# Router stage: second norm's shift by adding transfers, f32 router logits, another bank for the last projection, low parts later

## The chip, the cores and the metric

The kernel runs on one core of a Trainium2 chip. The core has five instruction queues that matter here: PE (TensorE, the matrix unit; PEld is its weight load), DVE (VectorE), ACT (ScalarE), POOL (GpSimd) and SP (SyncE, which here only issues transfers). Each works through its own instructions in order and waits for semaphores of the others. PSUM, where PE writes its results, has eight banks. The metric is the device time of one execution in microseconds (us), as the median of several runs.

## The reference

One layer of a diffusion transformer over 1024 tokens of width 1024, with a router and 16 experts. Each expert takes the 128 tokens that have the highest affinity for it.

```python
h = modulate(rmsnorm(x, g_mix), sh1, sc1)
... windowed attention and a short convolution over h @ w_in ...
x = x + gt1 * (concat([att, conv]) @ w_out)             # output projection

h2 = modulate(rmsnorm(x, g_ffn), sh2, sc2)              # second norm: r*g*(1+sc2) + sh2
aff = softmax(h2 @ w_router)                            # (1024, 16), float32
g, idx = top_k(aff.T, 128)                              # each expert picks 128 tokens
xs = h2[idx]                                            # gathered rows
a, u = xs @ w_gate, xs @ w_up
y = (silu(a) * u) @ w_down * g
x = x + gt2 * segment_sum(y, idx)                       # adds into the rows of the tokens
return rmsnorm(x, g_final)
```

## The kernel before

The kernel goes through the layer in stages. After the attention, a **router stage** goes over 8 tiles of 128 tokens (t = 0 to 7), and then an **expert stage** over 16 experts of three weight matrices each.

**The router stage.** `project(t)` multiplies tile t by `w_out` in 48 matmuls of 512 columns (L878; each product is split into a high part and low parts, three passes in all), adds the residual `xres` on DVE (L883, one operation for each half) and takes the root mean square. While PE works through `project(t)`, the work of the tile before it is woven in: `route(t-1)` turns `xres` by 8 PE transposes into bank `ph` (L951), copies it out of PSUM, multiplies it by the router's weights into logits `pl`, and takes the softmax into `aff`. Beside this, `finish_h2` makes the rows of the second norm: `h2 = x*S2` (`gained`, L887), then `h2*rstd + B2` (L933), and SP stores them to a DRAM tensor `h2_d`, 128 rows for each tile. S2 and B2 are the second norm's scale and shift as rows in SBUF.

For tiles 0 to 6 the logits are made in two steps: ACT copies `ph` as rounded high parts, DVE takes what is left as low parts (`x2s`, L956, two operations), PE multiplies both by the router's weights with the tokens as columns (`plT`, L970, 8 matmuls), ACT copies that out, and PE turns it back with two float32 matmuls (`pl`, L977). Tile 7, the last, is done otherwise: ACT copies `ph` as it is and PE multiplies it in plain float32 (L964, 8 matmuls, each of which shows as two records in the trace).

**Top 128 by sorting.** DVE holds the best 128 affinities of each of the 16 experts so far in a tile `L`. `sort(t0, n)` sorts the affinities of n tiles: PE turns them into a PSUM tile `pa` in bank p1(1), DVE copies that into `sa` (L1050, called the evict below) and then runs eight rounds of MAX8 and MATCH_REPLACE (L1057, L1059), followed by half cleaners (pairs of max and min, L1020 and L1021). `merge(t)` takes the maximum of `L` and the sorted list (L1077) and cleans `L` again with such pairs. Tiles 0 to 2 are sorted together, then 3 and 4, then 5, 6 and 7 alone. After `merge(7)`, `thr` is the smallest of the 128 (L1228). From it come a mask, the places of the chosen tokens, `idx` (L1275) and the gather of the rows of expert 0 from `h2_d` (POOL, L1310), the transposes of these rows (L1286) and the first expert matmul.

**The last tile.** For t = 7 the projection is split, so that the first half of the columns is ready early: 24 matmuls of 512 columns (L878), then two parts c = 0 and c = 1 with 24 matmuls of 256 columns each (L915). Part c = 0 writes to a half of bank pair p2(0); part c = 1 writes to bank p1(1), which is the bank of `pa`.

**The first weights.** The weights of expert 0 are split into a high part by ACT (L1145) and a low part by DVE (L1148) for each k of 8. `pre_split` does this ahead of the expert stage: k = 0, 1 and 2 whole, and the high part of k = 3. The low part of k = 3 stands between the mask of expert 1 and its `idx`.

**What sets the order.** In this stretch PE, SP, ACT and POOL work in the order in which the code is written out (a manual schedule); for DVE a scheduler places the instructions, and code marked as of high priority goes first.

Of the kernel before, what the change touches and what calls it, by code (L numbers as in the profile page):

```python
# [18 lines left out]
D = 1024  # L19
# [13 lines left out]
NW4 = 3  # L33

# [51 lines left out]
def tile_layer(ctx, tc, x, c, cx, c_ctx, w_ada, b_ada, g_mix, w_in, conv_w, sink, w_out, g_ffn,  # L86
# [751 lines left out]
    wmem = work.tile([128, 384], F32R, tag="mp", name="wrs")  # L838
    wrs, ident2 = shaped(wmem, (KC, 2, NE)), wmem[:32, 256:272].bitcast(F32)
    nc.vector.tensor_copy(wrs[:, :, 0], wr)  # L840
    nc.vector.tensor_tensor(wrs[:, :, 1], wr, wrs[:, :, 0].bitcast(F32), op=OP.subtract)
    nc.vector.tensor_tensor(wmem[:32, 256:272], ident[:32, 0:16], ident[:32, 16:32], op=OP.add)

    fold, sign = wmem[:, 272:336].bitcast(F32), wmem[:, 336:337].bitcast(F32)
    nc.vector.tensor_tensor(wmem[:, 272:336], ident[:, 0:64], ident[:, 64:128], op=OP.add)
# [16 lines left out]
    def project(t):  # L862
# [22 lines left out]
        def gained(cols):  # L885

            nc.vector.tensor_tensor(h2_of[t][:, cols], xt[:, cols], S2[:, cols], op=OP.mult)  # L887

        if t < NT - 1:
# [7 lines left out]
            gained(slice(0, D))  # L897
        else:
# [10 lines left out]
            po2 = [p2(0, "po")[:, 0], p1(1, "po")]  # L909
# [20 lines left out]
    def finish_h2(t):  # L930
        h2 = h2_of.pop(t)
        x2_of.pop(t)
        nc.vector.scalar_tensor_tensor(h2, h2, rstd[:, t:t + 1], B2, op0=OP.mult, op1=OP.add)  # L933
        h2_done[t] = h2
        if t < NT - 2:
            store_h2(t)
# [6 lines left out]
    def turn_x2(t, g, ks=None):  # L943
        if t < NT - 1:
            x2T_of[t, g] = (wm, w4)[g]("x2s", (4, 2, 128), F32R)
        elif g == 0:
            x2T_of[t] = wm("x2T")
        ks = ks or range(4 * g, 4 * g + 4)
        ph = p1(2 + ks[0] // 2 % 2 if t == NT - 1 else 2 + g, "ph")[:, 0:128 * len(ks)]
        for i, k in enumerate(ks):  # L950
            nc.tensor.transpose(ph[:, i * 128:(i + 1) * 128], x2_of[t][:, k * 128:(k + 1) * 128], ident)  # L951
        if t < NT - 1:
            hi, lo = [x2T_of[t, g][:, :, i] for i in range(2)]
            ph = ph.rearrange("p (a b) -> p a b", a=4)
            nc.scalar.copy(hi, ph)
            nc.vector.tensor_tensor(lo, ph, hi.bitcast(F32), op=OP.subtract)  # L956
        else:
            nc.scalar.copy(x2T_of[t][:, ks[0] * 128:(ks[-1] + 1) * 128], ph)
# [7 lines left out]
    def logits_T(t):  # L966

        pl = p1(0, "plT")
        for k in range(KC):
            mm(pl[:2 * NE, :256], wrs[:, k].rearrange("p a b -> p (a b)"),  # L970
               x2T_of[t, k // 4][:, k % 4].rearrange("p a b -> p (a b)"), start=k == 0, stop=k == KC - 1)
        lgT = work.tile([32, 256], F32, tag="up", name="lgT")
        nc.scalar.copy(lgT, pl[:32, :256])
        yield 0.8
        pl_of[t] = p1(0, "pl")
        for i in range(2):
            mm(pl_of[t][:, :NE], lgT[:, i * 128:(i + 1) * 128], ident2, start=i == 0, stop=i == 1)  # L977
# [223 lines left out]
    with order_of:  # L1201
# [19 lines left out]
        pre_split((2,))  # L1221
        split_rows("g", 0, 3, (0,))
# [307 lines left out]
```

## Time and profile before

| | us |
|---|---|
| median of 3 runs | 1177.36 (1175.39 to 1178.09) |
| the profiled execution, its own time | 1176.17 |
| its span in the trace | 1174.3 |
| PE busy | 1063.7 (91%) |
| DVE busy | 982.9 (84%) |
| ACT busy | 767.9 (65%) |
| POOL busy | 349.0 (30%) |

The busy shares are means over stages which have different limits. The router stage lies at about 440 to 580 us of the span, the expert stage at about 590 to 1130 us. In the profile's slices PE is at 9 tenths or more through the whole expert stage, and at less in the router stage's last part. All start times below are microseconds from the start of the span.

### The profile page before, as it was taken

The page shows a single profiled execution, that of the slowest core. Times are in us where ns is not written, and L with a number is a line of the kernel's source. Part 1 is how long each engine was busy: PE and PEld are TensorE (multiplying, and loading weights), DVE is VectorE, ACT ScalarE, POOL GpSimd, SP SyncE. Part 2 cuts the span into 40 slices and gives each one's busy share as a digit, 9 for nine tenths or more (in the row PEclk, how much of TensorE's full clock was granted, in tenths as well). Part 3 has the DMA queues.
Part 4 walks back from the last instruction along what each step waited for, and adds up shares of the span by engine and source line. Part 5 has one row for each costly group of instructions (what it writes and reads, how often), then busy time and mean ns, then how long its engine had stood idle before and what let it go on. Part 6 is the DMA issues. An engine that isn't in the chain of part 4 may idle for free.

```text
span 1174.3 us, 15578 instructions
## 1 busy us (share of the span) xinstructions
PE 1063.7 (91%) x5458; PEld 873.2 (74%) x5458; DVE 982.9 (84%) x1678; ACT 767.9 (65%) x1064; POOL 349.0 (30%) x288
## 2 busy tenths in 40 slices
PE   6786889999899998997399999999999999999982
PEld 2675667888787877776278888888888888888861
DVE  7887455887877786599879999999999999999985
ACT  7565545766666744232167888788888778788863
POOL 0457671211303031221204333223333223331022
PEclk9898999999999999999589999999999999999996
DMA  9644540100101175437579999999999999999646
GB/s 377 225 162 143 170 136 19 33 23 1 54 1 37 25 291 205 146 116 277 208 277 369 385 393 389 390 389 397 404 388 390 390 389 387 411 392 388 245 157 254
DMA packets 89638, 288.69 MB, mean 246 GB/s; under 512 B 6916, under 2 KB 20688, under 8 KB 88536
## 3 DMA queue, kind: packets, MB, share of 16 engines
q1 hardware_dynamic: 84808, 270.40, 60.6%
q0 software_dynamic: 4752, 17.30, 5.6%
q8 instruction: 43, 0.70, 0.2%
q14 instruction: 35, 0.29, 0.1%
HBM read 266.69 MB, written 20.99 MB: 245 GB/s over the span
## 4 chain that ended last, share of the span: by engine, by line
PE 71%; DVE 12%; DMA 7%; ACT 4%; issue 4%; POOL 1%; POOLq 0%; ACTq 0%; DVEq 0%; SPq 0%
PE pg L1300 15%; PE pu L1300 14%; PE py L1300 13%; PE po L878 5%; PE ps_cv L731 3%; PE ps_cv L730 3%; PE ps_cv L732 3%; PE pt L622 2%; PE po_att L613 2%; DMA xt<-in_x_dram 2%; PE ps_s L565 1%; PE xTp L1286 1%; PE ps_s L563 1%; PE hTtp L1286 1%; DMA wa<-in_w_ada_dram 1%
## 5 line engine op out<-in xcount | busy, mean ns | idle before, releaser
L1148 DVE TENSOR_TENSOR whl<-raw,whl 128x1024 fp32r<-128x1024 f32 x384 | 455.8, 1226 | 29.3 <-ACT whl L1145 18.5
L1145 ACT CAST whl<-raw 128x1024 fp32r<-128x1024 f32 x384 | 400.4, 1054 | 100.9 <-PE pu L1300 35.5
L1300 PE MATMUL pg<-whl,xT 128*128 128x512 f32 x768 | 187.0, 396 | 2.3 <-DVE whl L1148 2.3
L1300 PE MATMUL pu<-whl,xT 128*128 128x512 f32 x768 | 180.8, 391 | 0.0
L1300 PEld LDWEIGHTS pg<-whl,xT 128*128 128x128 f32 x768 | 142.7, 189 | 32.3 <-DVE whl L1148 3.2
L1300 PE MATMUL py<-whl,hTt 128*128 128x512 f32 x720 | 165.9, 389 | 0.0
L1300 PEld LDWEIGHTS pu<-whl,xT 128*128 128x128 f32 x768 | 143.1, 188 | 29.3
L1300 PEld LDWEIGHTS py<-whl,hTt 128*128 128x128 f32 x720 | 135.1, 188 | 28.3 <-DVE whl L1148 0.3
L1265 POOL TENSOR_SCALAR oh<-iota,pos 128x128 bf16<-128x128 f32 x108 | 103.7, 974 | 9.6 <-DVE pos L1250 9.1
L1358 POOL DMA_INDIRECT acc_d<-yt,idx x15 | 38.6, 2570 | 196.4 <-DVE yt L1346 196.4
L730 PE MATMUL ps_cv<-hTh,wcs 128*128 128x512 f32 x192 | 81.2, 423 | 0.0
L1310 POOL DMA_INDIRECT xr<-h_d,idx x16 | 21.8, 1361 | 189.7 <-DVE gate_w L1276 189.7
L463 POOL TENSOR_TENSOR acc<-acc,wmod 128x1024 f32<-128x1024 f32 x28 | 69.1, 2484 | 30.2 <-ACT wmod L461 29.8
L625 ACT CAST pth<-pt 128x512 fp32r<-128x512 f32 (+1 forms) x88 | 46.1, 524 | 46.1 <-PE pt L622 46.1
L731 PE MATMUL ps_cv<-hTl,wcs 128*128 128x512 f32 x192 | 76.1, 396 | 0.0
L732 PE MATMUL ps_cv<-hTh,wcs 128*128 128x512 f32 x192 | 76.0, 396 | 0.0
L626 DVE TENSOR_TENSOR pth<-pt,pth 128x512 fp32r<-128x512 f32 (+1 forms) x88 | 53.9, 614 | 20.2 <-ACT pth L625 19.0
L878 PE MATMUL po<-woh,ah 128*128 128x512 f32 x240 | 69.3, 403 | 0.6 <-ACT woh L223 0.6
L711 POOL TENSOR_TENSOR wcs<-wcr,wcs 128x1024 fp32r<-128x1024 f32 x12 | 28.6, 2390 | 110.4 <-ACT wcs L710 87.7
L578 ACT ACTIVATE sm<-sm,negm 128x640 f32<-128x640 f32 (+1 forms) x64 | 51.6, 807 | 3.9 <-DVE negm L577 3.8
L575 DVE CUSTOM_DVE_ANT_0 sm<-ps_s,maskt,sink 128x640 f32<-128x640 f32 (+1 forms) x56 | 48.4, 864 | 6.9 <-PE ps_s L565 6.3
L878 PEld LDWEIGHTS po<-woh,ah 128*128 128x128 f32 x240 | 44.4, 191 | 9.6 <-ACT woh L223 1.0
(292 smaller groups left out, 1843.2 us busy)
## 6 DMA issues: line engine op xcount, KB each, us to landing
raw<-in_w_gate_dram SPq DMA_DIRECT2D x64, 1024.0 KB, 10.1
raw<-in_w_up_dram SPq DMA_DIRECT2D x64, 1024.0 KB, 8.7
raw<-in_w_down_dram SPq DMA_DIRECT2D x64, 1024.0 KB, 10.2
wmod<-in_w_ada_dram SPq DMA_DIRECT2D x32, 512.0 KB, 3.8
wa<-in_w_ada_dram SPq DMA_DIRECT2D x8, 1024.0 KB, 5.4
wcr<-in_w_in_dram SPq DMA_DIRECT2D x12, 512.0 KB, 3.8
xt<-in_x_dram SPq DMA_DIRECT2D x4, 1024.0 KB, 20.6
wor<-in_w_out_dram SPq DMA_DIRECT2D x4, 1024.0 KB, 5.0
```

What stands on the lines that cost most here:

```text
L463: nc.gpsimd.tensor_tensor(acc, acc, wt, op=OP.add)
L575: nc.vector.tensor_tensor_reduce(dst, src, mk, op0=OP.add, op1=OP.max, scale=1.0, scalar=sink8[:, h:h + 1], accum_out=mx[:, b, h:h + 1])
L578: nc.scalar.activation(sm, sm, AF.Exp, bias=negm[:, b, h:h + 1], scale=0.125, accum_out=esum[:, b, h:h + 1])
L626: nc.vector.tensor_tensor(pth[:, 1, :n], pt[:, :n], pth[:, 0, :n].bitcast(F32), op=OP.subtract)
L730: mm(ps, wsp[:, 0, k], hi, start=k == 0, stop=False)
L731: mm(ps, wsp[:, 0, k], lo, start=False, stop=False)
L732: mm(ps, wsp[:, 1, k], hi, start=False, stop=k == KC - 1)
L878: mm(po[n], a, wo[k // 4, n][j][:, k % 4], start=first, stop=last)
L1145: nc.scalar.copy(w[:, 0], t[:, k % 2])
L1148: low = nc.vector.tensor_tensor(w[:, 1], t[:, k % 2], w[:, 0].bitcast(F32), op=OP.subtract)
L1265: nc.gpsimd.tensor_scalar(oh[:, t], iota1, pos[:, t, 0, e:e + 1], None, op0=OP.is_equal)
L1300: mm(ps[n], a_hl[:, a, k], w[:, j, n * 512:(n + 1) * 512], start=first, stop=last)
```

## The change

It has four parts.

1. **The second norm's shift.** For tiles 0 to 5 (`NADD = 6`) the rows of `h2_d` are first filled with B2 by six SP stores, early in the stage. `finish_h2` then makes `x*rstd*S2` in one DVE operation, and POOL adds these rows into `h2_d` by an indirect transfer with the row numbers `tokrow` (six small DVE operations). `gained` (L887) and SP's store of the tile are gone for these tiles. Tiles 6 and 7 stay as they were.
2. **The logits of tiles 0 to 6** are made as those of tile 7 were: ACT copies `ph` to `x2T`, PE multiplies in float32. L956, `plT`, its copy and the turn back are gone.
3. **The banks of the last projection.** Part c = 0 takes the second bank of the tile's own pair (`po[1]`), part c = 1 takes what c = 0 had. The bank of `pa` is used by `sort` alone.
4. **The low parts.** `pre_split` makes only the high parts of k = 0 to 3. The low parts of k = 0, 1 are written after the mask of expert 1, those of k = 2, 3 after `place` of the other experts.

```diff
+NADD = 6
...
+    tokrow = consts.tile([128, NT], I32, name="tokrow")
+    for t in range(NADD):
+        nc.vector.tensor_scalar(tokrow[:, t:t + 1], tokid, float(128 * t), None, op0=OP.add)
+        nc.sync.dma_start(h2_d[t * 128:(t + 1) * 128, :], B2)
...
-            gained(slice(0, D))
+            if t >= NADD:
+                gained(slice(0, D))
...
-            po2 = [p2(0, "po")[:, 0], p1(1, "po")]
+            po2 = [po[1], p2(0, "po")[:, 0]]
...
     def finish_h2(t):
-        h2 = h2_of.pop(t)
-        x2_of.pop(t)
-        nc.vector.scalar_tensor_tensor(h2, h2, rstd[:, t:t + 1], B2, op0=OP.mult, op1=OP.add)
-        h2_done[t] = h2
-        if t < NT - 2:
-            store_h2(t)
+        h2, xt = h2_of.pop(t), x2_of.pop(t)
+        if t < NADD:
+            nc.vector.scalar_tensor_tensor(h2, xt, rstd[:, t:t + 1], S2, op0=OP.mult, op1=OP.mult)
+            nc.gpsimd.indirect_dma_start(out=h2_d[:, :], out_offset=bass.IndirectOffsetOnAxis(ap=tokrow[:, t:t + 1], axis=0),
+                                         in_=h2, in_offset=None, compute_op=OP.add)
+        else:
+            nc.vector.scalar_tensor_tensor(h2, h2, rstd[:, t:t + 1], B2, op0=OP.mult, op1=OP.add)
+            h2_done[t] = h2
...
-        if t < NT - 1:
-            hi, lo = [x2T_of[t, g][:, :, i] for i in range(2)]
-            ph = ph.rearrange("p (a b) -> p a b", a=4)
-            nc.scalar.copy(hi, ph)
-            nc.vector.tensor_tensor(lo, ph, hi.bitcast(F32), op=OP.subtract)
-        else:
-            nc.scalar.copy(x2T_of[t][:, ks[0] * 128:(ks[-1] + 1) * 128], ph)
+        nc.scalar.copy(x2T_of[t][:, ks[0] * 128:(ks[-1] + 1) * 128], ph)
...
-            yield 1.3
-            yield from logits_T(t)
+            yield 1.6
+            logits(t, range(0, 4))
+            yield 0.9
+            logits(t, range(4, 8))
...
-            split_rows("g", 0, k)
+            split_rows("g", 0, k, (0,))
...
-        pre_split((2,))
-        split_rows("g", 0, 3, (0,))
+        pre_split((2, 3))
...
-    after(split_rows("g", 0, 3, (1,)), chosen)
+    for k in (0, 1):
+        after(split_rows("g", 0, k, (1,)), chosen)
...
     place(slice(2, NE))
+    for k in (2, 3):
+        after(split_rows("g", 0, k, (1,)), chosen)
```

The lines of the changed kernel are numbered a little otherwise: L915 becomes L917, L964 becomes L960, L1048 and L1050 become L1033 and L1035, L1148 becomes L1133.

On PE, at the end of the last tile's part c = 0 (`po<-woh_4065` and `po<-wol_4066`) and the first matmul of part c = 1 (`po<-woh_4011`), with the transpose for the sort of tile 6 (`pa`) and logits of tile 7 (`pl`). Before:

```order
L915 MATMUL po<-wol_4066,ah_5052 128x256
L1048 MATMUL pa<-wrs,affh 64x64
L915 MATMUL po<-woh_4065,ah_5052 128x256
L964 MATMUL pl<-wr,x2T 128x16 x4
L915 MATMUL po<-woh_4065,ah_5052 128x256
L915 MATMUL po<-wol_4066,ah_5052 128x256
L915 MATMUL po<-woh_4065,ah_5052 128x256
L915 MATMUL po<-woh_4011,ah_5052 128x256
```

After:

```order
L917 MATMUL po<-woh_4065,ah_5008 128x256
L960 MATMUL pl<-wr,x2T 128x16 x4
L917 MATMUL po<-woh_4065,ah_5008 128x256
L917 MATMUL po<-wol_4066,ah_5008 128x256
L917 MATMUL po<-woh_4065,ah_5008 128x256
L1033 MATMUL pa<-wmem,affh 64x64
L917 MATMUL po<-woh_4011,ah_5008 128x256
```

The transpose for the sort of tile 6 has moved behind the last matmul of part c = 0, and the first matmul of part c = 1 still follows at once, but into another bank than `pa`.

On DVE, from the residual of tile 6 (`xres<-po`, 128x512 x2) on, with the sort of tile 5 (`sa<-pa`, then MAX and MATCH_REPLACE). Before:

```order
L883 TENSOR_TENSOR xres<-po,xres 128x512 x2
L1020 TENSOR_TENSOR L<-L 16x2x32
L1021 TENSOR_TENSOR L<-L 16x2x32
L1050 TENSOR_SCALAR sa<-pa,wrs 64x64
L1020 TENSOR_TENSOR L<-L 16x4x16
L1021 TENSOR_TENSOR L<-L 16x4x16
L1057 MAX ss<-sa 64x8
L1020 TENSOR_TENSOR L<-L 16x8x8
L1021 TENSOR_TENSOR L<-L 16x8x8
L1059 MATCH_REPLACE sa<-ss,sa 64x64
```

After, up to that residual (now L884):

```order
L1035 TENSOR_SCALAR sa<-pa,wmem 64x64
L1005 TENSOR_TENSOR L<-L 16x4x16
L1006 TENSOR_TENSOR L<-L 16x4x16
L1042 MAX ss<-sa 64x8
L1005 TENSOR_TENSOR L<-L 16x8x8
L1006 TENSOR_TENSOR L<-L 16x8x8
L1044 MATCH_REPLACE sa<-ss,sa 64x64
L1005 TENSOR_TENSOR L<-L 16x16x4
L1006 TENSOR_TENSOR L<-L 16x16x4
L1042 MAX ss<-sa 64x8
L1005 TENSOR_TENSOR L<-L 16x32x2
L1006 TENSOR_TENSOR L<-L 16x32x2
```

The evict and the first two rounds of the sort of tile 5 stood behind the residual of tile 6 and stand ahead of it now.

On DVE, between the `idx` of expert 0 (`idx<-pi`, with `gate_w` behind it) and that of expert 1, with the mask (`oh`) of expert 1 and the first low parts (`whl`). Before:

```order
L1275 TENSOR_REDUCE idx<-pi 128x1
L1276 TENSOR_REDUCE gate_w<-pi 128x1
L1261 TENSOR_TENSOR oh<-iota_2951,pos 128x768
L1148 TENSOR_TENSOR whl_5356<-raw_4095,whl_5356 128x1024
L1275 TENSOR_REDUCE idx<-pi 128x1
L1276 TENSOR_REDUCE gate_w<-pi 128x1
L1249 TENSOR_TENSOR pos<-pf,M 128x16x14
```

After:

```order
L1259 TENSOR_REDUCE idx<-pi 128x1
L1260 TENSOR_REDUCE gate_w<-pi 128x1
L1245 TENSOR_TENSOR oh<-iota_2951,pos 128x768
L1133 TENSOR_TENSOR whl_5058<-raw_4103,whl_5058 128x1024
L1133 TENSOR_TENSOR whl_5196<-raw_4103,whl_5196 128x1024
L1133 TENSOR_TENSOR whl_5298<-raw_4105,whl_5298 128x1024
L1133 TENSOR_TENSOR whl_5300<-raw_4105,whl_5300 128x1024
L1259 TENSOR_REDUCE idx<-pi 128x1
L1260 TENSOR_REDUCE gate_w<-pi 128x1
L1233 TENSOR_TENSOR pos<-pf,M 128x16x14
```

Where one low part stood ahead of the `idx` of expert 1, all four stand now.

## Rows read from the trace of the kernel before

**Rows 1.** Windows: length, busy PE, PEld, DVE, ACT, POOL, clock, DMA share, GB/s.

```profile
454.00:482.00 28.00, 28.00 (x143) 22.88 (x142) 13.60 (x26) 8.15 (x19) 5.58 (x12) 1.00 0.48 162
...
557.00:564.00 7.00, 6.48 (x32) 6.13 (x32) 6.31 (x42) 0.74 (x3) 0.00 (x0) 0.61 0.00 0
...
616.00:1120.00 504.00, 504.00 (x2431) 416.89 (x2430) 479.74 (x478) 406.09 (x422) 152.38 (x132) 1.00 0.99 379
```

**Rows 2.** Timeline, last projection: start, duration, engine, line, tiles, idle time before and releaser.

```profile
556.57 0.27 DVE L1050 TENSOR_SCALAR sa<-pa,wrs 64x64 f32<-64x64 f32 x1
...
556.89 0.58 PE L915 MATMUL po<-woh,ah 128*128 128x256 f32 x1 [6.83 <-DVE sa L1050]
...
563.17 0.42 DVE L919 TENSOR_TENSOR xres<-po,xres 128x256 f32<-128x256 f32 x1 [0.25 <-PE po L915]
```

**Rows 3.** Timeline, PE: first transposes of tiles 3 and 6.

```profile
495.24 1.03 PE L951 MATMUL ph<-ident,xres 128*128 128x128 f32 x8
...
538.06 1.03 PE L951 MATMUL ph<-ident,xres 128*128 128x128 f32 x8
```

**Rows 4.** Chain of waits in the router stage: start, duration, step.

```profile
459.24 0.54 PE pl L977 x4
...
468.19 0.87 PE ph L951 x8
...
484.46 0.94 PE plT L970 x8
```

**Rows 5.** Timeline, PEld, the float32 logits of tile 7.

```profile
548.53 0.98 PEld L964 LDWEIGHTS pl<-wr,x2T 128*128 128x128 f32 x8
```

**Rows 6.** Timeline, DVE, from the residual of tile 6 to the sort of tile 6.

```profile
536.44 1.29 DVE L883 TENSOR_TENSOR xres<-po,xres 128x512 f32<-128x512 f32 x2 [0.51 <-PE po L878]
...
538.97 1.20 DVE L887 TENSOR_TENSOR h<-xres,rowsA 128x1024 f32<-128x1024 f32 x1
...
540.51 1.26 DVE L956 TENSOR_TENSOR x2s<-ph,x2s 128x512 fp32r<-128x512 f32 x2
...
544.35 1.21 DVE L1148 TENSOR_TENSOR whl<-raw,whl 128x1024 fp32r<-128x1024 f32 x1
...
551.36 0.41 DVE L887 TENSOR_TENSOR h<-xres,rowsA 128x256 f32<-128x256 f32 x1
...
557.17 0.19 DVE L1020 TENSOR_TENSOR L<-L 16x64 f32<-16x64 f32 x1
...
558.76 0.21 DVE L1057 MAX8 ss<-sa 64x8 f32<-64x64 f32 x1
```

**Rows 7.** Timeline, DVE, from the merge of tile 6 to the threshold.

```profile
567.10 0.28 DVE L1077 SCALAR_TENSOR_TENSOR L<-sa,L 16x128 f32<-16x128 f32 x1
...
569.23 0.27 DVE L1050 TENSOR_SCALAR sa<-pa,wrs 64x64 f32<-64x64 f32 x1
...
570.32 1.20 DVE L1148 TENSOR_TENSOR whl<-raw,whl 128x1024 fp32r<-128x1024 f32 x1
...
578.61 0.27 DVE L1228 TENSOR_REDUCE thr<-L 16x1 f32<-16x128 f32 x1
```

**Rows 8.** Timeline, from the first gather to the first expert's operand.

```profile
583.44 1.73 POOL L1310 DMA_INDIRECT xr<-h_d,idx  x1 [0.75 <-DVE gate_w L1276]
...
586.76 0.16 DVE L1275 TENSOR_REDUCE idx<-pi 128x1 int32<-128x2 f32 x1 [1.36 <-PE pi L1273]
...
587.72 0.39 DVE L1249 TENSOR_TENSOR pos<-pf,M 128x224 f32<-128x224 f32 x1 [0.73 <-PE pf L1248]
...
590.44 0.69 DVE L1289 TENSOR_TENSOR xT<-xTp,xT 128x512 fp32r<-128x512 f32 x1 [0.69 <-ACT xT L1288]
```

**Rows 9.** The adding transfers of the expert stage: landing times (answer for L1358, 15 transfers).

```profile
DMA to landing us min/median/max: 10.0/10.2/12.7
```

**Rows 10.** Timeline beside such a transfer's issue on POOL.

```profile
639.91 3.49 DVE L1148 TENSOR_TENSOR whl<-raw,whl 128x1024 fp32r<-128x1024 f32 x3
...
640.28 2.37 POOL L1358 DMA_INDIRECT acc_d<-yt,idx  x1 [11.27 <-DVE yt L1346]
```

More of the change, by code (lines that the diff above doesn't have):

```diff
@@ L836, in tile_layer @@
     triu, iota1, tokid, wr, lbias = [rt[k] for k in ('triu', 'iota1', 'tokid', 'wr', 'lbias')]
[L838 to L845, printed above, removed]
+    wmem = work.tile([128, 384], F32, tag="mp", name="wmem")
+    fold, sign = wmem[:, 0:64], wmem[:, 64:65]
+    nc.vector.tensor_tensor(fold, ident[:, 0:64], ident[:, 64:128], op=OP.add)
+    tokrow = consts.tile([128, NT], I32, name="tokrow")
+    for t in range(NADD):
+        nc.vector.tensor_scalar(tokrow[:, t:t + 1], tokid, float(128 * t), None, op0=OP.add)
+        nc.sync.dma_start(h2_d[t * 128:(t + 1) * 128, :], B2)
     for i in range(4):
@@ L943, in turn_x2 @@
     def turn_x2(t, g, ks=None):
-        if t < NT - 1:
-            x2T_of[t, g] = (wm, w4)[g]("x2s", (4, 2, 128), F32R)
-        elif g == 0:
+        if g == 0:
             x2T_of[t] = wm("x2T")
@@ L951, in turn_x2 @@
             nc.tensor.transpose(ph[:, i * 128:(i + 1) * 128], x2_of[t][:, k * 128:(k + 1) * 128], ident)
-        if t < NT - 1:
-            hi, lo = [x2T_of[t, g][:, :, i] for i in range(2)]
-            ph = ph.rearrange("p (a b) -> p a b", a=4)
-            nc.scalar.copy(hi, ph)
-            nc.vector.tensor_tensor(lo, ph, hi.bitcast(F32), op=OP.subtract)
-        else:
-            nc.scalar.copy(x2T_of[t][:, ks[0] * 128:(ks[-1] + 1) * 128], ph)
+        nc.scalar.copy(x2T_of[t][:, ks[0] * 128:(ks[-1] + 1) * 128], ph)
     def logits(t, ks):
@@ L964, in logits @@
             mm(pl_of[t][:, :NE], x2T_of[t][:, k * 128:(k + 1) * 128], wr[:, k, :], start=k == 0, stop=k == KC - 1)
[L966 to L977, printed above, removed]
     def route(t):
```

## The prediction

> **What bounds the kernel now.** I read the busy time by windows first. In the expert stage PE works for 504.00 of 504.00 us, so whatever makes that stage begin earlier moves the end one to one, and nothing in the change touches the stage itself [rows 1]. The question is when the first expert matmul can start, and that depends on the chain that ends in the threshold `thr` at 578.61 [rows 7]. So I followed this chain backwards in the timelines of PE and DVE.
>
> Early in the router stage, PE is the limit: 28.00 of 28.00 us from 454 on, with DVE at 13.60 [rows 1]. From the transposes of tile 1 to those of tile 3 two tiles pass, 468.19 to 495.24 or 13.53 each; from tile 3 to tile 6 it is 14.27 each (538.06 less 495.24, over 3), because there the sorts lie on DVE as well and PE waits for the low parts of `x2s` [rows 3, 4]. At the end PE stands still for 6.83 us: the first matmul of part c = 1 wants bank p1(1), in which `pa` of the sort of tile 6 still lies, and DVE copies `pa` out only at 556.57, since it has the sort of tile 5 and its merge before it [rows 2]. Part c = 1 then runs at a mean granted clock of 0.61, mostly at the lower of the two levels (1.2 of 2.4 GHz), after that pause [rows 1]. Its residual at 563.17 opens the way to the softmax of tile 7, its sort (evict at 569.23) and the last merge [rows 2, 7].
>
> **The change part by part.** All times are those of the trace of before; a minus is a gain.
>
> *Logits on PE.* Per tile 8 `plT` matmuls (0.94) and the turn back (0.54) go, 1.48 together [rows 4]. Plain float32 shows two records for a matmul; tile 7's eight took 0.98, so a whole tile of 16 is 1.96 [rows 5]: +0.48. From below, the price could be 1.48 if records pipeline with the projection as `plT` does (+0); from above, the four records of `pl` took 0.54, which makes 16 cost 2.16 (+0.68) [rows 4]. I take +0.48, since tile 7's is the same operation between the same neighbours. In the tiles up to 3 PE is the limit, so three tiles of logits (0 to 2) give +1.44 by tile 3's transposes. After that the 0.74 by which these tiles were longer (14.27 less 13.53) goes with `x2s`, which PE waited for: 3 × (0.48 − 0.74) = −0.78. Tile 6's transposes come 0.66 later, and tile 7's first part ends 0.66 − 0.26 = 0.4 later: 550.06 (556.89 less 6.83 [rows 2]) becomes 550.46.
>
> *The shift.* For tiles 0 to 5, DVE loses `gained` (1.20) and keeps one operation of the size that it had [rows 6]. SP's six stores of B2 stand where SP waits for free weight buffers, and the transfer engines are 0.48 busy there [rows 1]: 0 on the path; without that cover they would delay the next load by a few us, but no matmul of the stage waits for it. The adding transfer costs POOL an issue of 2.37, and 10.0 to 12.7 us to land [rows 9, 10]. The next one writes the same tensor, so it waits on POOL's queue until that landing, and behind it stand `vals` and the next tile's inverse root (`rstd`). A tile takes 13.5 to 14.3 us [rows 3], so the landing is hidden with 1 to 3 us to spare: 0. The gather is at 583.44, far behind the last of them [rows 8].
>
> *DVE up to the evict of tile 6.* From the end of tile 6's residual (536.44 + 1.29 = 537.73 [rows 6]) to the evict at 556.57 are 18.84 us [rows 2], in which DVE nearly never rests. Out of it go: both `x2s` of tile 6, 1.26; two low parts like the one at 544.35, at 1.16 each where DVE is full (3.49 for three [rows 10]), 2.32; the evict and two rounds of tile 5's sort, which stand ahead of the residual now, because tiles 3 to 5 have 1.26 + 1.20 us less on DVE each: 2.19, by the same piece of the sort of tile 6 (556.57 to 558.76 [rows 2, 6]); and the last `gained` quarter, 0.41, which stands behind the evict [rows 6]. 12.66 are left, from 538.39 (0.66 late): 551.05. On PE the transpose to `pa` comes behind part c = 0: 550.46, about 0.3 for the transpose and 0.25 until DVE sees it [rows 2], 551.0. Both ways meet; I take 551.3 for the evict, **−5.3**.
>
> *The bank.* Part c = 1 doesn't wait any more. It took 6.28 from 556.89 to the residual [rows 2] at clock 0.61; at full clock (2.4 GHz) that is 6.28 × 0.61 = 3.83. From 550.8 it ends at 554.6, 8.6 sooner. The full 8.6 is not had, since the sort of tile 7 needs the merge of tile 6 done on DVE: softmax and the rest took 569.23 − 563.17 = 6.06 behind the residual [rows 2, 7], so tile 7's logits would be ready for the sort at about 561, and the merge isn't done by then.
>
> *DVE from the evict of tile 6 to the threshold.* Evict to merge took 10.53 (567.10 [rows 7]); +0.41 for the quarter moved here, +0.35 more wait for the residual of c = 1 (0.25 before [rows 2], about 0.6 now): 562.6, −4.5. From the merge to the evict of tile 7 took 2.13, as DVE waited for tile 7's logits; these are early now, so 0.3 is left: 562.9, −6.3. From there to `thr` took 9.38 [rows 7]. The low part at 570.32 goes (1.16), and four more pairs of half cleaners from the merge stand behind the evict. A pair is two rows of 0.2 [rows 6], of which between nothing (in the gaps of the sort) and 0.4 counts, 0 to 1.6 for four; I take 0.6, as rounds with and without pairs alternate. 8.82: `thr` at 571.7, **−6.9**.
>
> *Counted the other way:* what leaves DVE between 537.73 and `thr` is 1.26 + 3 × 1.16 + 2.19 = 6.93, and it begins 0.66 later. So the gain is 6.3 plus what idle time goes, if DVE is the limit throughout. The two counts agree within 0.6.
>
> *The low parts after the threshold.* From `thr` to the gather nothing changes. Behind it, three more low parts, 3 × 1.16 = 3.48, stand ahead of the `idx` of expert 1, on DVE where it waited 1.36, 0.73 and 0.69, together 2.78 [rows 8]. That hides all but 0.70; without this cover it would be 3.48. **+0.7**.
>
> Sum: −6.9 + 0.7 = −6.2. Against the profiled execution (1176.17, span 1174.3) that is 1170.0 and 1168.1; the median of before lies 1.2 above the profiled one, and I put the forecast at **1177.36 − 6.2 = 1171.2**.
>
> A rule that speaks against the change: while POOL issued an adding transfer for 2.37, DVE did three low parts, each with two inputs in SBUF, in 3.49, no longer than anywhere else [rows 10]. The Trainium skill (SBUF — State Buffer, section SBUF: two separate sides) says that a DVE operation with two SBUF inputs and a GpSimd operation that reads SBUF share a port pair as an exclusive lock, and that the other "fully blocks". By the row it costs nothing here; by that rule it gives rival 4.
>
> **The rivals.**
> 1. *DVE ends last.* Tiles 3 to 6 stay at 14.27 and take the 0.48 of the logits as well: tile 6's transposes are then 1.44 + 1.44 = 2.88 late instead of 0.66, and everything on DVE 2.2 later: −4.0. If half of the cover of the low parts (1.4) fails too, −2.6. For it: DVE is busy for almost the whole of these tiles [rows 6]. Against it: 2.46 us leave it per tile. 1173 to 1175.5; I name 1174.0.
> 2. *All of the wait is had.* Tile 7's chain (−8.6) ends last rather than the merge, and the low part (1.16) goes behind it: −8.6 − 1.16 + 0.7 = −9.1: 1168.3. Against it: the merge of tile 6 (562.6) lies behind the point at which tile 7 would be ready (561).
> 3. *No effect.* Rival 1, with the two rounds of tile 5's sort not hidden ahead of the residual (2.19): −6.2 + 2.2 + 2.2 and half the cover gone (1.4) is −0.4: 1177.0. So the bank's wait would be replaced by a wait for DVE.
> 4. *Issue and DVE exclude each other.* Three transfers, tiles 3 to 5, × 2.37 = 7.1 on a full DVE [rows 10]; tiles 0 to 2 have room (13.60 of 28.00 [rows 1]). −6.2 + 7.1 = +0.9: 1178.3. The row above speaks against it.
> 5. *Slower: the float32 logits.* If their weight loads don't overlap the projection and a tile's 16 records cost twice the row, 3.92 instead of 1.96, tiles 0 to 6 pay 7 × 1.96 = 13.7, and the time is 1177.36 − 6.2 + 13.7 = 1184.9. It decides from 6.2 / 7 = 0.9 us per tile over my price. Against it: both other rows, at most 0.2 above [rows 4].
> 6. *Slower: the landing.* If a transfer into `h2_d` lands in more than a tile's 13.5, POOL's queue, with the next `rstd` in it, runs at that rate: at 16 us, 5 × 2.5 = 12.5 and 1183.7. It turns into a loss from 13.5 + 6.2 / 5 = 14.7. Fifteen transfers of this kind took 12.7 at most, among heavier traffic (0.99 against 0.48 [rows 1, 9]).
>
> **How the numbers follow.** Forecast 0.55, rival 1 0.18, rival 2 0.06, rival 3 0.08, rival 4 0.04, rival 5 0.05, rival 6 0.04. About 0.2%, or 2.35 us, is what a measurement of this kernel tells from no change. Faster by over that: the forecast, rival 2 and most of rival 1 (0.14), 0.75. Within it: the rest of rival 1 (0.04), rival 3 and most of rival 4 (0.03), 0.15. Slower: rivals 5 and 6 and the rest, 0.10. The range's lower end is rival 2 with a little of the logits' lower bound, 1168.0. The upper end covers rival 1 and half of rival 3, 1177.0; what lies beyond is about 0.18.
>
> **What would show it.** Right, if in the trace of the changed kernel the first matmul of c = 1 follows that of `pa` without a wait for DVE, the evict of tile 6 lies near 551.3, that of tile 7 directly behind the merge of tile 6 near 563, `thr` near 571.7, and the first expert matmul some 6 us sooner. The logits are right if a tile's 16 records take about 2 us, and tiles 3 to 6 are about 14.0 apart. The low parts are right if the four in a row cost the first expert's operand under 1 us. Wrong, if tiles 3 to 6 grow (rivals 1, 3 and 5), if POOL waits for a landing with `rstd` behind it (rival 6), or if DVE stops while POOL issues (rival 4).

## The result and the profile after

The changed kernel takes 1169.34 us in the median of 4 runs (1168.05 to 1169.71), the kernel before 1176.51 beside it (4 runs). The ratio is 0.9937, with a 95% interval of 0.9921 to 0.9953: 5.5 to 9.3 us faster, where 6.2 were forecast. The profiled execution took 1168.05, its span is 1166.3.

The whole says little about single steps, since the stretch ahead of the router stage varies: tile 0's transposes began at 454.48 in the trace of before and at 452.00 here, although that stretch holds the same work except for some small operations. In two traces of the changed kernel the steps *inside* the router stage agreed within 0.02 us, each of them. So I compare step by step, each from one mark to the next:

| step, us | before | prediction | after |
|---|---|---|---|
| transposes of tile 0 to those of tile 3 | 40.76 | 42.20 | 40.98 |
| tile 3 to tile 6 | 42.82 | 42.04 | 41.15 |
| to the evict of tile 6 | 18.51 | 12.58 | 12.45 |
| to the merge of tile 6 | 10.53 | 11.3 | 11.85 |
| to the evict of tile 7 | 2.13 | 0.3 | 0.38 |
| to `thr` | 9.38 | 8.82 | 8.78 |
| to the gather | 4.83 | 4.83 | 4.88 |
| to the first expert matmul | 7.02 | 7.7 | 8.54 |
| **sum** | **135.98** | **129.8** | **129.01** |
| from there to the end | 583.84 | 583.84 | 585.29 |

(The prediction's column is its own marks, one less the other.) The router stage is 6.97 shorter. With 1.45 more behind it and 2.48 less ahead of it, that makes the 8.0 by which the two spans differ.

The two ends of the sum on PE in the trace of before, the first transposes of tile 0 and the first expert matmul; between them, the transposes of tile 1:

```profile
454.48 1.03 PE L951 MATMUL ph<-ident,xres 128*128 128x128 f32 x8
...
468.03 1.03 PE L951 MATMUL ph<-ident,xres 128*128 128x128 f32 x8
...
590.46 1.65 PE L1300 MATMUL pg<-whl,xT 128*128 128x512 f32 x3
```

The timeline of PE after, at the first transposes of tiles 0, 2, 3 and 6, at tile 2's logits with the matmul behind them, and at the first expert matmul; it answers to [rows 3] and [rows 4]:

```profile
452.00 1.03 PE L953 MATMUL ph<-ident,xres 128*128 128x128 f32 x8
...
479.24 1.03 PE L953 MATMUL ph<-ident,xres 128*128 128x128 f32 x8
...
481.97 0.96 PE L960 MATMUL pl<-wr,x2T 128*128 128x16 f32 x8
482.78 0.70 PE L879 MATMUL po<-woh,ah 128*128 128x512 f32 x2
...
492.98 1.03 PE L953 MATMUL ph<-ident,xres 128*128 128x128 f32 x8
...
534.13 1.03 PE L953 MATMUL ph<-ident,xres 128*128 128x128 f32 x8
...
581.01 1.22 PE L1284 MATMUL pg<-whl,xT 128*128 128x512 f32 x2
```

Eight records of the float32 logits hold PE for 482.78 less 481.97, 0.81 us. A tile has two such groups, 1.62, where `plT` and the turn back took 1.48 [rows 4]. From tile 3 to tile 6 a tile takes 13.72 (41.15 over 3), nearly what the tiles before them take in this trace (13.62 to 13.74).

The beginning and the end of part c = 0 on PE, with `pa` and the first matmuls of part c = 1; it answers to [rows 2]. The last line is the transpose for the sort of tile 7:

```profile
541.42 0.39 PE L917 MATMUL po<-woh,ah 128*128 128x256 f32 x1 [0.78 <-DVE xres L884]
...
545.65 0.28 PE L917 MATMUL po<-woh,ah 128*128 128x256 f32 x1
545.86 0.33 PE L1033 MATMUL pa<-wmem,affh 128*64 128x64 f32 x2
546.12 0.39 PE L917 MATMUL po<-woh,ah 128*128 128x256 f32 x1
...
555.28 0.48 PE L1033 MATMUL pa<-wmem,affh 128*64 128x64 f32 x2 [3.35 <-DVE affh L984]
```

Part c = 1 follows without a wait, and ahead of the evict. It takes 3.81 from its first matmul to its residual (549.93 below), where the prediction had 3.83. The new bank has a small wait of its own: part c = 0 now waits 0.78 for DVE's residual of the first half, which reads the other bank of the same pair; before, it followed at once. On DVE, the residuals of both parts, the evict and the merge of tile 6, the evict of tile 7 and the threshold (as [rows 2, 6, 7]):

```profile
545.97 0.42 DVE L921 TENSOR_TENSOR xres<-po,xres 128x256 f32<-128x256 f32 x1
...
546.58 0.27 DVE L1035 TENSOR_SCALAR sa<-pa,wmem 64x64 f32<-64x64 f32 x1
...
549.93 0.43 DVE L921 TENSOR_TENSOR xres<-po,xres 128x256 f32<-128x256 f32 x1 [0.55 <-PE po L917]
...
558.43 0.28 DVE L1062 SCALAR_TENSOR_TENSOR L<-sa,L 16x128 f32<-16x128 f32 x1
...
558.81 0.28 DVE L1035 TENSOR_SCALAR sa<-pa,wmem 64x64 f32<-64x64 f32 x1
...
567.59 0.27 DVE L1212 TENSOR_REDUCE thr<-L 16x1 f32<-16x128 f32 x1
```

The evict of tile 7 follows the merge of tile 6 at once; its transpose on PE was done at 555.76, 2.7 earlier. Behind the threshold, on POOL, PE and DVE, from the gather to the first transposes of the operand (as [rows 8]; `oh` on POOL are the two slices of expert 1's one-hot mask that POOL makes; the line of 4.72 is all four low parts together, the second and the third of which also stand alone):

```profile
572.47 1.63 POOL L1294 DMA_INDIRECT xr<-h_d,idx  x1 [0.72 <-DVE gate_w L1260]
573.15 4.72 DVE L1133 TENSOR_TENSOR whl<-raw,whl 128x1024 fp32r<-128x1024 f32 x4
...
574.14 1.77 POOL L1249 TENSOR_SCALAR oh<-iota,pos 128x128 bf16<-128x128 f32 x1
574.29 1.22 DVE L1133 TENSOR_TENSOR whl<-raw,whl 128x1024 fp32r<-128x1024 f32 x1
575.43 1.31 DVE L1133 TENSOR_TENSOR whl<-raw,whl 128x1024 fp32r<-128x1024 f32 x1
575.90 2.36 POOL L1249 TENSOR_SCALAR oh<-iota,pos 128x128 bf16<-128x128 f32 x1
575.97 0.19 PE L1257 MATMUL pi<-vals,oh 128*128 128x8 bf16 x1 [2.48 <-POOL oh L1249]
578.32 0.19 PE L1257 MATMUL pi<-vals,oh 128*128 128x8 bf16 x1 [2.16 <-POOL oh L1249]
...
578.54 0.16 DVE L1259 TENSOR_REDUCE idx<-pi 128x1 int32<-128x2 f32 x1 [0.68 <-PE pi L1257]
```

This is a wait that was not in the prediction. In the kernel before, the two slices of expert 1 began at the end of the one low part and took 1.26 together:

```profile
585.22 1.26 POOL L1265 TENSOR_SCALAR oh<-iota,pos 128x128 bf16<-128x128 f32 x2
```

Beside four low parts in a row on DVE they take 4.12 (1.77 and 2.36), and PE waits 2.48 and 2.16 for them, with the operand's transposes queued behind. The first slice ends 0.40 behind the end of the second low part (575.51), and the second one 0.39 behind the end of the fourth (577.87).

### The profile page after: what moved, and what is told of

Read it like the earlier page. It is cut to its first block, busy times and chain, and to the rows that moved or that the text cites. A ratio compares the mean times of both kernels' runs of the same rounds, so it can differ in the third digit from the quotient of the medians.

```text
span 1166.3 us, 15621 instructions
## 1 busy us (share of the span) xinstructions
PE 1061.0 (91%) x5486; PEld 875.6 (75%) x5486; DVE 966.0 (83%) x1661; ACT 765.4 (66%) x1057; POOL 353.3 (30%) x294
## 4 chain that ended last, share of the span: by engine, by line
PE 71%; DVE 11%; DMA 7%; ACT 4%; issue 4%; POOL 2%; POOLq 0%; ACTq 0%; DVEq 0%; SPq 0%
PE pg L1284 14%; PE pu L1284 14%; PE py L1284 13%; PE po L879 6%; PE ps_cv L732 3%; PE ps_cv L731 3%; PE ps_cv L733 3%; PE pt L623 2%; PE po_att L614 2%; DMA xt<-in_x_dram 2%; PE ps_s L566 2%; PE xTp L1270 1%; DVE whl L1133 1%; PE ps_s L564 1%; PE hTtp L1270 1%
## 5 line engine op out<-in xcount | busy, mean ns | idle before, releaser
L1133 DVE TENSOR_TENSOR whl<-raw,whl 128x1024 fp32r<-128x1024 f32 x384 | 455.2, 1224 | 30.5 <-ACT whl L1130 19.6
L1249 POOL TENSOR_SCALAR oh<-iota,pos 128x128 bf16<-128x128 f32 x108 | 106.7, 1002 | 13.3 <-DVE pos L1234 12.8
```

Source lines behind the costliest of these rows:

```text
L1133: low = nc.vector.tensor_tensor(w[:, 1], t[:, k % 2], w[:, 0].bitcast(F32), op=OP.subtract)
L1249: nc.gpsimd.tensor_scalar(oh[:, t], iota1, pos[:, t, 0, e:e + 1], None, op0=OP.is_equal)
```

## The experiments

All of them are read by the steps above. "Stage" is the time from tile 0's transposes to the first expert matmul: 135.98 before, 129.01 after.

**The banks alone, on the kernel before.**

```diff
-            po2 = [p2(0, "po")[:, 0], p1(1, "po")]
+            po2 = [po[1], p2(0, "po")[:, 0]]
```

> The kernel before, with only the banks of the last projection changed (part c = 0 in the second bank of the tile's own pair, part c = 1 in the bank that c = 0 had). Theory S (DVE sets the chain to the threshold): part c = 1 ends about 7 us sooner, but the evict of tile 6 and the merge of tile 6 stay where they are, because DVE's work before them is the same; only the 2.1 us from that merge to the evict of tile 7 shrink to about 0.4. Gain 1.7 us, about 1174.8 against 1176.5. Rival W (the wait of PE is itself the path): the 6.8 us of the wait come through, about 1169.7.

Ratio 0.9994 (0.9985 to 1.0002), stage 134.99, so 0.99 of 6.97. On DVE, the last residual, the evict of tile 6, its merge, and the evict of tile 7:

```profile
553.00 0.42 DVE L919 TENSOR_TENSOR xres<-po,xres 128x256 f32<-128x256 f32 x1
...
554.99 0.27 DVE L1050 TENSOR_SCALAR sa<-pa,wrs 64x64 f32<-64x64 f32 x1
...
566.34 0.28 DVE L1077 SCALAR_TENSOR_TENSOR L<-sa,L 16x128 f32<-16x128 f32 x1
566.73 0.28 DVE L1050 TENSOR_SCALAR sa<-pa,wrs 64x64 f32<-64x64 f32 x1
```

The last residual comes 17.15 behind tile 6's transposes (535.85 in this trace) instead of 25.11, 8 us sooner, and the wait of 6.83 is gone. But the evict comes 19.14 behind them and the merge 30.49, where they came 18.51 and 29.04 before: both are later, as the residual of part c = 1 and more of tile 7's operations now stand ahead of them on DVE. So the gain is 0.99 instead of the 1.7 that I expected. Theory S holds in what it says of the cause: PE waited because DVE was late, and freeing PE alone does not make DVE earlier.

**The banks undone, in the changed kernel** (the same edit the other way round).

> The changed kernel, with the banks of the last projection as before (part c = 1 in the bank of pa). Theory S: pa is written behind part c = 0 now and copied out at 546.6, when PE has just come to part c = 1; the wait is under 1 us instead of 6.8, and the time is 0 to 1 us above the changed kernel, 1169.3 to 1170.3. Rival W: the wait comes back and most of the gain goes, about 1175.

Ratio 0.9946 (0.9933 to 0.9958), stage 129.79, 0.78 slower than the changed kernel. The wait is there again, but short:

```profile
548.73 0.58 PE L917 MATMUL po<-woh,ah 128*128 128x256 f32 x1 [2.10 <-DVE sa L1035]
```

It is 2.10 long, where I had expected under 1, and short against 6.83, since the evict itself is early in this kernel. Part c = 1 then runs at a mean granted clock of 0.53 from 549 to 552. The effect on the whole is as Theory S had it.

**The low parts early, in the changed kernel.**

```diff
-            split_rows("g", 0, k, (0,))
+            split_rows("g", 0, k)
...
-        pre_split((2, 3))
+        pre_split((2,))
+        split_rows("g", 0, 3, (0,))
...
-    for k in (0, 1):
-        after(split_rows("g", 0, k, (1,)), chosen)
+    after(split_rows("g", 0, 3, (1,)), chosen)
...
-    for k in (2, 3):
-        after(split_rows("g", 0, k, (1,)), chosen)
```

> The changed kernel, with the low parts of k = 0 to 2 early, as before. Theory S: three low parts of 1.16 us go back into DVE's work ahead of the threshold, some of it into gaps (0.5 to 1 us), so the threshold comes 2.5 to 3.5 us later; from the gather to the first expert matmul 8.5 us shrink to 7.0, so the whole is 1 to 2 us slower, 1170.3 to 1171.3. Rival: the low parts found room in DVE's gaps, the threshold moves by under 1 us, and the time is 1168 or less.

Ratio 0.9960 (0.9946 to 0.9974), stage 130.07, 1.06 slower. The threshold comes 2.97 later behind tile 6's transposes (36.43 instead of 33.46), and from the gather to the first expert matmul there are 6.70 instead of 8.54. So this part of the change gives 2.97 and takes 1.84 back (the thr-to-gather step differs by 0.07), and what it takes back is in good part the wait for POOL's slices (0.97, by the run with the mask on DVE below).

**The old logits, in the changed kernel.**

```diff
-            yield 1.6
-            logits(t, range(0, 4))
-            yield 0.9
-            logits(t, range(4, 8))
+            yield 1.3
+            yield from logits_T(t)
```

(with `x2s`, `wrs` and `logits_T` as they were)

> The changed kernel, with the logits of tiles 0 to 6 as before (rounded high parts and low parts, plT, its copy, the turn back). Theory S (DVE's work ahead of the threshold sets the gain): the two x2s operations, 1.26 us for a tile, come back on DVE. Tiles 0 to 3 become 0.1 shorter each on PE (13.53 instead of 13.62), tiles 3 to 6 stay near 13.7 or grow to 14.0, and from tile 6's transposes to the evict of tile 6 there are 1.3 us more: 1.0 to 2.5 us slower than the changed kernel, 1170.4 to 1171.9. Rival P (float32 logits are dear on PE, and DVE has room): the same or faster, 1168.5 to 1169.5.

Ratio 0.9991 (0.9977 to 1.0005), stage 134.40: 5.39 of the 6.97 are gone, far more than either theory said. The tiles grew to 14.15 on the first step and 14.26 on the next two. From the timeline of this kernel, DVE's two `x2s` (L964), the second norm's operation (L939) and PE's `plT` (L978):

```profile
485.28 0.69 DVE L964 TENSOR_TENSOR x2s<-ph,x2s 128x512 fp32r<-128x512 f32 x1 [2.04 <-ACT x2s L963]
...
485.89 1.27 DVE L939 SCALAR_TENSOR_TENSOR h<-xres,rstd,rowsA 128x1024 f32<-128x1024 f32 x1
...
486.76 0.63 PE L978 MATMUL plT<-x2s,wrs 128*32 128x256 f32 x4
487.08 0.68 DVE L964 TENSOR_TENSOR x2s<-ph,x2s 128x512 fp32r<-128x512 f32 x1
...
487.81 0.66 PE L978 MATMUL plT<-x2s,wrs 128*32 128x256 f32 x4 [0.42 <-DVE x2s L964]
```

The second norm's operation reads `xres` itself now, so it can start as soon as `rstd` is there, and the scheduler places it between the two `x2s`. PE then waits for the second one. To test that, **the same with that operation held behind the second `x2s`** (`x2s_last[t]` is the second `x2s` of tile t):

```diff
-            nc.vector.scalar_tensor_tensor(h2, xt, rstd[:, t:t + 1], S2, op0=OP.mult, op1=OP.mult)
+            after(nc.vector.scalar_tensor_tensor(h2, xt, rstd[:, t:t + 1], S2, op0=OP.mult, op1=OP.mult), x2s_last[t])
```

> The variant with the old logits, in which the second norm's one operation on DVE stood between the two x2s operations (tiles were 14.15 to 14.6 us long there). Here that operation is made to wait for the second x2s. Theory O (the order on DVE makes the tiles longer: plT waits for the second x2s behind an operation of 1.28 us): tiles 0 to 3 come back to 13.55 to 13.65, tiles 3 to 6 to 13.7 to 14.0, and tile 0's transposes to the first expert matmul take 130 to 131.5 us instead of 134.4. Rival P (with the adding transfers PE or POOL needs the time itself): the tiles stay over 14.1.

Ratio 0.9951 (0.9934 to 0.9968), two runs of this one kernel. The tiles are 13.56, then 13.60, then 13.64 long, and the stage is 131.49. So 2.91 of the 5.39 were the order on DVE, and 2.48 are what the float32 logits are worth when the order is right. From tile 6's transposes to the evict of tile 6 there are 16.14 here and 12.45 in the changed kernel; of these 3.69, the tiles ahead give 0.45 back, and the step up to the merge 0.77.

**No adding transfers, in the changed kernel.**

```diff
-NADD = 6
+NADD = 0
...
             h2_done[t] = h2
+            if t < NT - 2:
+                store_h2(t)
```

> The changed kernel, with all tiles of the second norm made as before (NADD = 0: x*S2, then *rstd + B2, stored by SP; no rows prepared, no adding transfers). Theory S: 1.20 us come back on DVE for each of six tiles; tiles 3 to 6 grow by 0 to 0.4 each and one round of tile 5's sort falls behind the residual of tile 6 (0.9): 0.5 to 2 us slower in the router stage. Theory T (the loads of the accumulated rows at the very end take 10.0 to 10.5 us in all kernels with adding transfers in the router stage, 8.9 in the two without, and the adding transfers are the cause): the end comes 1.3 us sooner after the last transposes, so the whole is -0.8 to +0.7 against the changed kernel. Rival to T (the loads' time is by chance or comes from the timing of the end): they stay at 10 and more.

Ratio 0.9962 (0.9948 to 0.9976), stage 130.20: the adding transfers are worth 1.19 of the stage, and nearly all of it lies between tile 6's transposes and the evict (14.24 instead of 12.45, of which 0.68 come back up to the merge). The tiles are as long as in the changed kernel (41.14 for three). Theory T fell: the first expert matmul to the end takes 584.83 here, and the last loads take 10.2 us as well.

**The logits alone, on the kernel before** (the edit of the logits as in the diff of the change, nothing else).

> The kernel before, with plain float32 logits alone. Price on PE: tiles 1 to 3 are 13.62 apart instead of 13.53 if a tile's 16 records cost what the changed kernel's trace shows (8 records in 0.81 us), 14.0 if they cost the 0.48 of the prediction. Theory S: tiles 3 to 6, 14.27 apart before, come to 13.7; from tile 6's transposes to the evict of tile 6 there are 18.5 - 1.3 us, less what of tile 5's sort moves ahead of the residual of tile 6 (0.9), about 16.3; the wait of part c = 1 for the bank stays at 4 to 5 us; the threshold comes 3 to 4.5 us sooner than in the kernel before: about 1173. Rival W (only the bank's wait counts): no gain, 1176.5.

Ratio 0.9998 (0.9986 to 1.0010), stage 132.34, which is 3.64 shorter than before. The tiles are 13.61, 13.70 and 13.71 long, as expected, and PE still waits 5.81 for the bank. That the whole does not show the 3.64 is not explained by the stage: in its profiled execution tile 0's transposes came at 456.34 (1.86 later than before), and from the first expert matmul to the end there are 585.12 (1.28 more). The first of these two may belong to the execution alone: in the two traces of the spread variant below, which is one kernel, tile 0's transposes came at 456.15 and 452.30. But 12 runs show nothing of the 3.64 in the median, and that stays unexplained.

**The adding transfers alone, on the kernel before.**

> The kernel before, with the second norm's shift by adding transfers alone (old logits, old banks, low parts early). Theory O: the one operation of the second norm lands between the two x2s, tiles 0 to 3 grow from 13.55 to about 14.15 and tiles 3 to 6 from 14.27 to about 14.5, 2.5 us up to tile 6's transposes; behind them nothing is gained but one or two rounds of tile 5's sort (0.9 to 2.2). So -0.5 to +1.5 us, 1176 to 1178. Rival S (1.20 us less on DVE for each tile come through): 2 to 4 us faster.

Ratio 1.0004 (0.9995 to 1.0014), stage 136.14: no gain. From tile 0 to tile 6 there are 86.34 instead of 83.58, by the same order on DVE, and 2.28 less from there to the evict. Alone, this part makes a new wait that eats what it saves.

**The mask of expert 1 on DVE, in the changed kernel** (no slices on POOL).

```diff
-        n = (NT - 2 if e < 2 else NT) if e < 3 else 0
+        n = (NT - 2 if e < 1 else NT) if e < 3 else 0
```

> The changed kernel, with the whole one-hot mask of expert 1 on DVE (1.23 us instead of 0.95) and no slices of it on POOL. Theory C (the slices stood behind DVE's four low parts): PE's two waits for them (2.5 and 2.2 us) are gone, but the idx of expert 1 still stands behind the four low parts on DVE (4.7 us), so from the gather to the operand's transposes 6.8 becomes 6.3 to 6.5, and the whole is 0.3 to 0.5 faster: 1168.8 to 1169.1. In the spread variant both had gone, and there it was 5.1. Rival: the slices are what counts, 5.1 here as well, 1167.7.

Ratio 0.9942 (0.9927 to 0.9957), stage 128.03. The `idx` of expert 1 follows the four low parts at once:

```profile
575.49 4.63 DVE L1133 TENSOR_TENSOR whl<-raw,whl 128x1024 fp32r<-128x1024 f32 x4
575.51 0.37 PE L1257 MATMUL pi<-vals,oh 128*128 128x8 bf16 x8 [1.45 <-DVE oh L1245]
580.04 0.15 DVE L1259 TENSOR_REDUCE idx<-pi 128x1 int32<-128x2 f32 x1
580.36 1.94 PE L1270 MATMUL xTp<-ident,xr 128*128 128x128 f32 x8 [3.51 <-DVE gate_w L1260]
```

PE is done with `pi` at 575.9 and with the places (`pf`) at 576.85, and then waits 3.51 for DVE. From the gather to the operand's transposes there are 5.82 instead of 6.79: 0.97 was the slices on POOL, twice what I expected, and what is left above the 5.11 of the next run is the order on DVE. From the gather to the first expert matmul there are 7.58, 0.56 more than before, close to the 0.7 of the prediction, which had counted DVE's work and not POOL's. The four low parts take 4.63 without POOL's slices beside them and 4.72 with them, so DVE loses 0.09 where POOL's two slices take 4.12 instead of 1.26.

**The low parts spread, in the changed kernel.**

```diff
-    for k in (0, 1):
-        after(split_rows("g", 0, k, (1,)), chosen)
+    after(split_rows("g", 0, 0, (1,)), chosen)
     idx1 = choose(1)
+    after(split_rows("g", 0, 1, (1,)), idx1)
...
-    place(slice(2, NE))
+    placed = place(slice(2, NE))
     for k in (2, 3):
-        after(split_rows("g", 0, k, (1,)), chosen)
+        after(split_rows("g", 0, k, (1,)), placed)
```

> The changed kernel, with the four low parts spread: k = 0 behind the mask of expert 1, k = 1 behind the idx of expert 1, k = 2 and 3 behind the places of the other experts. Theory C (POOL's two one-hot slices of expert 1 stood 4.1 us instead of 2.0 beside the four low parts on DVE, and PE waited 2.5 and 2.2 us for them): with one low part beside them the slices take about 1 us each, with a little more for the first, and from the gather to the first expert matmul there are 7.0 to 7.3 us instead of 8.5: 1.2 to 1.5 us faster, about 1168.0. Rival (the operand's landing or the low parts themselves set the start): no change, 1169.3.

Ratio 0.9941 (0.9926 to 0.9956), stage 127.36, 1.65 shorter than the changed kernel's. From the gather on, with one low part beside the slices, and in the last line a matmul a little behind the first expert matmul:

```profile
577.32 1.22 DVE L1133 TENSOR_TENSOR whl<-raw,whl 128x1024 fp32r<-128x1024 f32 x1
...
578.31 1.31 POOL L1249 TENSOR_SCALAR oh<-iota,pos 128x128 bf16<-128x128 f32 x2
579.09 0.19 PE L1257 MATMUL pi<-vals,oh 128*128 128x8 bf16 x1 [1.42 <-POOL oh L1249]
579.68 0.19 PE L1257 MATMUL pi<-vals,oh 128*128 128x8 bf16 x1 [0.41 <-POOL oh L1249]
...
586.20 10.27 PE L1284 MATMUL pg<-whl,xT 128*128 128x512 f32 x44 [0.91 <-DVE xT L1273]
```

The slices take 1.31 instead of 4.12, and the operand's transposes come 5.11 behind the gather. The stage bears Theory C out. The whole did not show it there, so **the changed kernel and this variant ran once more, side by side**:

> The changed kernel once more, beside the spread variant on the same chip. The steps from tile 0's transposes to the first expert matmul are the same as in its first trace within 0.1 us (129.0 together); the stretch before them and the end vary from one execution to the next, by 1 to 2 us.

> The variant with the low parts spread (k = 0 behind the mask of expert 1, k = 1 behind its idx, k = 2 and 3 behind the places of the other experts), beside the changed kernel. Theory C: from the gather to the operand's transposes 5.1 instead of 6.8, and the whole 1.0 to 1.7 us faster than the changed kernel. Rival: what is gained there is lost in the first expert's pass, and the two are within 0.5 us.

The changed kernel: ratio 0.9955 (0.9941 to 0.9969), median 1170.13 of 6. The spread variant: 0.9943 (0.9930 to 0.9956), median 1168.27 of 5. The stages are 129.0 and 127.3, the same as in their first traces within 0.1. The spread variant is 1.7 shorter in the stage, but the stage's end mark flatters it. The first expert matmul begins sooner, and four matmuls on PE waits 0.91 (1.06 in the second trace) for DVE's half of the operand (`xT`), which now stands behind the last low parts. From the first expert matmul to the end this variant takes 586.30 and 585.93, the changed kernel 585.29 and 585.16. So from tile 0's transposes to the end it is 0.6 and 0.9 shorter, and the rival of this run, that the gain is lost in the first expert's pass, is right in part: 0.5 and 0.6 of it are lost by the last expert's transposes of the hidden layer. By the whole time the two intervals overlap; the highest and lowest of the 6 runs of the changed kernel lie 5.3 apart.

## Why the prediction came out right, and where its steps were off

1. **What bounds it** (DVE's work up to the threshold, counted in both ways): right, and the runs bear it out. The bank's wait of 6.83, the most visible idle time of the profile, was worth 0.99 by itself and 0.78 at the end of the change.
2. **The logits on PE**: sign right, size wrong. The prediction took +0.48 for a tile, from 1.96 against 1.48 [rows 4, 5]; it is +0.14, and a tile grew by 0.07, from 13.55 to 13.62 between tile 0 and tile 1. The 0.98 of [rows 5] is the duration of a group of weight loads (PEld), with its last record's tail in it; the 0.94 and 0.54 of [rows 4] are steps of a chain, from one piece to the next. Unlike things were subtracted. On PE the same group of tile 7 took 0.81 from its first matmul to the next one of the projection (548.65 to 549.46 in the trace of before). That alone is 1.2 us at tile 3, and the mistake made the prediction 1.2 too slow there.
3. **Tiles 3 to 6**: right in kind (what `x2s` cost went with it), 13.72 instead of 14.01, again because the logits cost less. The 0.74 has the same mistake in it: 468.19 is a piece of the chain, and tile 1's transposes begin at 468.03, so the tiles before tile 3 took 13.60 rather than 13.53, and the excess was 0.67.
4. **Up to the evict of tile 6**: 12.58 forecast, 12.45 measured. This term carried the forecast and was taken apart by rows, operation by operation. The runs that put work back on DVE bear it out: the step is 14.07 with the low parts early, 14.24 without the adding transfers and 16.14 with the old logits in the right order.
5. **To the merge of tile 6**: 1.32 more than before instead of 0.77. Two steps of tile 7's softmax moved ahead of the merge (to 554.49 and 554.76), as tile 7 is early now. In the kernel before they stood behind it (567.10 [rows 7]), in the 2.13 that I had let go:

```profile
567.69 0.14 DVE L995 RECIPROCAL sc<-sc 128x1 f32<-128x1 f32 x1
568.07 0.46 DVE L999 TENSOR_SCALAR affh<-aff,sc 64x16 f32<-64x16 f32 x2
```

   That is the kernel before; together 0.6, about the 0.55 that was missed. No run tests this by itself. What is said to be "idle" between two marks can hold work that only changes sides.
6. **To the threshold**: 8.82 forecast, 8.78 measured.
7. **The low parts behind the threshold**: +0.7 forecast, +1.5 measured. The count of DVE's time was right (4.72 for four), and its idle time of 2.78 was there. What failed is the cover: the low parts were laid beside work that was taken to be DVE's and PE's, and POOL's two slices stood in it too. With them gone from POOL the step is +0.56 (7.58 against 7.02).
8. **The adding transfers**: right. Six issues of 1.62 to 1.79, landing 5.8 to 8.5 us after the issue, well within a tile; no wait for a landing stands ahead of `rstd`. Rival 6 is out. In the timeline after, one such issue beside DVE's half cleaners:

```profile
509.66 1.62 POOL L936 DMA_INDIRECT h_d<-h,tokrow  x1 [1.61 <-DVE L L1006]
509.67 0.25 DVE L1005 TENSOR_TENSOR L<-L 16x64 f32<-16x64 f32 x1
509.84 0.21 DVE L1006 TENSOR_TENSOR L<-L 16x64 f32<-16x64 f32 x1
510.08 0.21 DVE L1005 TENSOR_TENSOR L<-L 16x64 f32<-16x64 f32 x1
```

   DVE's operations go on at about their usual 0.21 through it, so rival 4 is out as well: here an issue costs DVE nothing. Three of the six issues ran beside small operations like these and three beside an idle DVE; beside low parts there is only [rows 10], where the issue took 2.37 and DVE lost nothing either. The Trainium skill's rule that the prediction weighed (SBUF — State Buffer, section SBUF: two separate sides) shows in another place: POOL's slices, which read SBUF, took 1.77 and 2.36 us beside low parts with two SBUF inputs each, where a slice of expert 0 with DVE idle took 0.59 (571.15 in the same trace), with starts of PE's dependent matmuls 2.35 apart, two low parts. There the trace agrees with it in that POOL waited through whole operations of DVE. DVE itself hardly waited: the low part that ran at the end of the first slice took 1.31 instead of 1.22.
9. **Rivals 1 and 3** (DVE late from tile 3 on) are out for the change as a whole, since tiles 3 to 6 shrank to 13.72. But the mechanism exists: with the old logits, the adding transfers bring tiles of 14.15 to 14.65, and alone they gain nothing. Rival 2 is out, since tile 7 was ready for its sort 2.7 us before the merge of tile 6. Rival 5 is out, since a tile's logits hold PE for 1.62 and not for 3.92.

The sum of the misses: 1.22 and 0.89 too slow at the tiles, 0.13 at the evict, 0.55 and 0.08 too fast at the merge, 0.04 back and 0.05 on to the gather, 0.82 too fast behind it. That is 0.78, the difference between 6.19 and 6.97. That the forecast of the stage came within 1 us is in part luck, by this cancelling: 2.28 too slow in one place, 1.50 too fast in another. And 2.48 of the 8.0 between the two profiled executions lie ahead of the stage, where nothing was forecast.

**What stays open.** From the first expert matmul to the end the changed kernel took 585.29 and 585.16, before 583.84. It lies behind the last expert's transposes of the hidden layer: from there to the end 34.3 before, 35.8 after, where the loads of the accumulated rows took 8.9 before and 10 or more in most of the later kernels. Only the banks alone kept 34.5; all others took 35.0 to 36.4. It is not the adding transfers, since it is there without them; its cause was not found. The granted clock moves this stretch too: in the first 4 us of the expert stage its mean was 0.67 before, 0.59 after, and 0.86 in the run with the operation held behind `x2s`, which has 583.85 from there to the end although its last part takes 35.0.

## What to carry to other kernels

- The longest idle time on an engine names who is late, and is not itself the price. Taking away the wait of 6.83 alone gave 1.0; with the bank as before, taking work off the engine that was waited for still gave 6.2 of the 7.0.
- Parts of a change are not a sum: the adding transfers alone gave nothing, with the float32 logits 1.2, since the shorter dependence let a scheduler put an operation between two that PE wants. After an operation loses an input, look where it has moved to.
- Subtract like from like: steps from start to start, not durations of groups. And "hidden beside idle time" has to be checked for every engine in that stretch, POOL too.
- A stage that ends sooner can hand its wait on. Look a few instructions behind the mark to which the gain is counted, as the spread variant shows.

## What the runs showed of the hardware

- A slice of the mask on POOL (128 elements in each of 128 partitions) took 0.59 with DVE idle, and 1.77 and 2.36 beside four low parts in a row, each time ending 0.4 behind the end of a low part. Two slices took 1.26 to 1.39 where a single low part of DVE ended beside them. The four low parts themselves took 4.72 instead of 4.63.
- An adding transfer's issue on POOL (1.62) beside DVE's small operations (16x64 elements) cost DVE nothing: 0.21 to 0.25 each.
- In the changed kernel part c = 1 ran at the full clock, 2.4 GHz (granted clock 1.00 from 541 to 549.5), where PE had paused for under 1 us, and with the banks alone also (1.00 from 544.5 to 553), where PE had paused for 1.43 ahead of part c = 0. After the pause of 6.83 it ran at 0.61 [rows 1], and with the banks undone, after a pause of 2.10, at 0.53 from 549 to 552.
